# A weighted sum over eight experts on one core: the weights come in transfers of 121 and of 7 partitions instead of 128

## The chip, the core and the metric

The kernel runs on one core of a Trainium2 chip. The time is the device time of one execution in microseconds (us); lower is better. Seven executions of the kernel before took 707.96 to 708.42 us, with a median of 708.09 us.

## What is computed

```python
batch, seq, n_experts, expert_dim = 16, 1024, 8, 512
expert_outputs   # (16, 1024, 8, 512) float32
combine_weights  # (16, 1024, 8) float32

def reference(expert_outputs, combine_weights):
    weights = combine_weights[..., np.newaxis]
    return np.sum(expert_outputs * weights, axis=2).astype(np.float32)
```

There are 16 x 1024 = 16384 tokens. Each has eight rows of 512 numbers and eight weights, and its output is the weighted sum of its eight rows. The input is 268 MB, the output 33.6 MB, and the weights are 0.5 MB, so nearly all that moves is `expert_outputs`, once, and it is used once.

## The kernel before

**Tiling.** The tokens are laid on 128 partitions, 128 tokens on each. 120 of them are done in a loop, the last 8 (`TAIL`) behind it. The loop has 12 rounds (`ROUNDS`) of 10 tokens for each partition (`R`). The input of one round fills a buffer `ring` in SBUF, and it comes in three transfers (`CHUNKS`) of 4, 4 and 2 tokens for each partition: 8.4, 8.4 and 4.2 MB. A chunk of the next round overwrites the same place as soon as VectorE has used it.

**The order of transfers.** SyncE (`SP` in the profile) issues the loads in a fixed order, written out in `loads_and_last_stores`. Ahead of each load it waits for the semaphore `done`, which VectorE counts up for each finished token. After the first chunk of the first round, SyncE issues the two transfers of the weights: the 120 tokens of the loop (three runs of 1280 bytes for each partition, L113) and the 8 of the tail (256 bytes for each partition, L116). Both count up `w_in` when they land. Then come the rest of the loads, the eight loads of the tail (L119, one token each), and the last five stores (L99, L123). ScalarE (`ACT`) issues the eleven other stores from its own queue, one for each round (L99).

**The weights.** ScalarE waits for `w_in`, then copies the weights of each round from `w_t` to `w_c` (L145), two rounds in turn, and counts up `w_set`. In the tail it multiplies an identity matrix by a column of weights (L151), which TensorE uses.

**The sum.** VectorE does the loop: for each token a product (L204) and seven fused multiply-adds (L187), two tokens interleaved. Ahead of a round it waits for the weights and for the store of two rounds ago, and ahead of a chunk for its landing (all with L173). In the tail TensorE sums the first four experts of each token in PSUM (L163, with the diagonal matrices as weights) and VectorE adds the other four. VectorE waits for `w_in` once more before the tail.

**DMA engines.** Sixteen DMA engines serve the core. A transfer over 128 partitions is split into sixteen shares of eight partitions, each engine takes its share in the order of the queue, and adds one to the semaphore when its share has landed; the transfer has landed when sixteen have come.

## Time and profile before

| | |
|---|---|
| median of seven executions | 708.09 us (707.96 to 708.42) |
| the profiled execution: its own time | 707.74 us |
| its span in the profile | 705.9 us |
| VectorE busy | 628.2 us (89%) |
| TensorE, ScalarE, GpSimd busy | 33.4, 16.7, 0.7 us |
| DMA: moved, mean rate | 302.53 MB, 429 GB/s |
| packets on SyncE's queue (q1), ScalarE's (q10), instructions' (q14) | 7600, 1584, 2 |
| mean granted TensorE clock | 0.994 |

The span is the stretch that the profile shows; the 1.84 us between it and the execution's own time lie around it. The profiled execution is 0.35 us below the median of the seven. In the profile's rows of slices a digit is the share of time in tenths, 9 being 90% or more. A "packet" is what one DMA engine moves in one go: 64 KB of one partition for a chunk of four tokens, 20 KB for a store, 1280 bytes for a run of weights, 4 bytes for the count of a semaphore. The trace holds queue, start, duration and size of each packet and the time of each of the sixteen counts of a transfer, but not the number of the DMA engine.

### The profile page before, as it was taken

Reading aid. Unit: us, or ns where it says so; the run is one execution under the profiler, and the core shown is the slowest. Engines: PE = TensorE matmul, PEld = TensorE weight load, DVE = VectorE, ACT = ScalarE, POOL = GpSimd, SP = SyncE. Lnnn points to the kernel's source line nnn. Section 1 sums busy time; section 2 is a strip of 40 time slices with the busy share of each in tenths; the row PEclk is TensorE's granted clock in tenths of the full one; section 3 lists DMA queues with packets and bytes.
Section 4 is the critical chain, followed back from the end, with each engine's and each line's share of the span. In section 5 each row is a group of like instructions: output and inputs, shape, how many; then the busy total and the mean of one; then the engine's idle time right before and its main releaser. Section 6 shows DMA issues by size and latency. Waiting matters only on the chain. (4 is left out here: it accounts for less than half of the span.)

```text
span 705.9 us, 1388 instructions
## 1 busy us (share of the span) xinstructions
PE 33.4 (5%) x64; PEld 13.2 (2%) x64; DVE 628.2 (89%) x992; ACT 16.7 (2%) x45; POOL 0.7 (0%) x6
## 2 busy tenths in 40 slices
PE   0000000000000000000000000000000000000674
PEld 0000000000000000000000000000000000000221
DVE  0599989979979979979979989998997997997995
ACT  0000000000000000000000000000000000000221
POOL 0000000000000000000000000000000000000000
PEclk9999999999999999999999999999999999999998
DMA  9999999999999999999999999999999999999997
GB/s 408 394 472 420 401 429 447 412 446 420 450 431 451 431 405 446 436 424 470 434 396 454 417 425 436 472 395 467 420 446 416 427 430 457 434 432 402 429 430 331
DMA packets 9186, 302.53 MB, mean 429 GB/s; under 512 B 1120, under 2 KB 1504, under 8 KB 1888
## 3 DMA queue, kind: packets, MB, share of 16 engines
q1 hardware_dynamic: 7600, 273.68, 90.0%
q10 hardware_dynamic: 1584, 28.84, 9.5%
q14 instruction: 2, 0.02, 0.0%
HBM read 268.96 MB, written 33.55 MB: 429 GB/s over the span
## 5 line engine op out<-in xcount | busy, mean ns | idle before, releaser
L187 DVE SCALAR_TENSOR_TENSOR acc<-ring,w_c,acc 128x512 f32<-128x512 f32 x840 | 561.4, 744 | 0.0
L204 DVE TENSOR_SCALAR acc<-ring,w_c 128x512 f32<-128x512 f32 x120 | 52.6, 480 | 68.2 <-DVEq L173 68.2
L163 PE MATMUL ps<-ring,diag 128*128 128x512 f32 x64 | 33.4, 676 | 663.9 <-DMA ring<-in_expert_outputs_dram 663.8
L163 PEld LDWEIGHTS ps<-ring,diag 128*128 128x128 f32 x64 | 13.2, 214 | 683.2 <-DMA ring<-in_expert_outputs_dram 668.3
L187 DVE SCALAR_TENSOR_TENSOR acc<-ring,w_t,acc 128x512 f32<-128x512 f32 x24 | 17.6, 749 | 0.6
L145 ACT COPY w_c<-w_t 128x80 f32<-128x80 f32 x12 | 3.0, 258 | 560.0 <-DVE acc L187 537.7
L151 ACT ACTIVATE diag<-ident,w_t 128x128 f32<-128x128 f32 x32 | 12.4, 400 | 114.6 <-PE ps L163 60.4
L187 DVE SCALAR_TENSOR_TENSOR acc<-ring,w_t,ps 128x512 f32<-128x512 f32 x8 | 5.9, 742 | 3.4 <-PE ps L163 3.4
L145 ACT ACT_TABLE_LOAD x1 | 1.3, 1283 | 0.9 <-SPq L230 0.9
L129 POOL TENSOR_SCALAR_AFFINE_SELECT ident<-ident 128x128 f32<-128x128 f32 x1 | 0.3, 292 | 0.1
L128 POOL MEMSET ident<- 128x128 f32 x1 | 0.2, 204 | 0.5 <-SPq L230 0.5
L250 POOL MEMSET const-bfloat16-1.0<- 128x1 bf16 x1 | 0.1, 101 | 0.0
L250 POOL MEMSET const-uint8-127<- 128x1 uint8 x1 | 0.1, 101 | 0.0
L250 POOL MEMSET const-float32-0.0<- 128x1 f32 x1 | 0.1, 98 | 0.2 <-issue 0.2
L250 POOL MEMSET const-float32-1.0<- 128x1 f32 x1 | 0.1, 98 | 0.0
## 6 DMA issues: line engine op xcount, KB each, us to landing
ring<-in_expert_outputs_dram SPq DMA_DIRECT2D x12, 4096.0 KB, 34.4
out_dram<-acc ACTq DMA_DIRECT2D x11, 2560.0 KB, 26.7
ring<-in_expert_outputs_dram SPq DMA_DIRECT2D x8, 2048.0 KB, 30.1
out_dram<-acc SPq DMA_DIRECT2D x1, 2560.0 KB, 26.2
out_dram<-acc SPq DMA_DIRECT2D x1, 1024.0 KB, 16.4
out_dram<-acc SPq DMA_DIRECT2D x1, 512.0 KB, 9.5
out_dram<-acc SPq DMA_DIRECT2D x2, 256.0 KB, 5.4
w_t<-in_combine_weights_dram SPq DMA_DIRECT2D x1, 480.0 KB, 22.7
```

Source lines behind the costliest of these rows:

```text
L128: gpsimd.memset(ident, 0.0).then_inc(id_set, 1)
L129: gpsimd.affine_select(out=ident, in_=ident, compare_op=mybir.AluOpType.not_equal, fill=1.0, base=0, pattern=[[-1, P]], channel_multiplier ...
L145: scalar.copy(out=w_c[:, h * R : h * R + R], in_=w_t[:, n * R : n * R + R]).then_inc(w_set[h], 1)
L151: i = scalar.mul(out=diag[:, k % DIAGS], in_=ident, mul=w_t[:, LOOP + j, e : e + 1])
L163: tensor.matmul(ps[:, j], lhsT=diag[:, k % DIAGS], rhs=ring[:, j, e], start=e == 0, stop=e == pe_e[j] - 1,).then_inc(product, 1)
L187: return vector.scalar_tensor_tensor(out=acc[:, g], in0=ring[:, g % R, e], scalar=weight, in1=before, op0=mult, op1=add)
L204: i = vector.tensor_scalar_mul(out=acc[:, g], in0=ring[:, g % R, 0], scalar1=weight)
L250: nc = _bacc.Bacc("TRN2", target_bir_lowering=False, num_devices=1)
```

## The change

Each of the two transfers of the weights becomes two: one for partitions 0 to 120, and one for partitions 121 to 127. 121 partitions are split over eleven DMA engines with eleven partitions each, seven over seven engines with one each. The order on SyncE's queue is 121 partitions of the loop's weights, 121 of the tail's, 7 of the loop's, 7 of the tail's; they stand at the same place between the first and the second chunk. The two waits for `w_in` wait for 64 instead of 32. SyncE issues two more transfers; no other engine's instructions change.

```diff
                 if n == 0 and c == 0:
-                    sync.dma_start(
-                        out=w_t[:, 0:LOOP].rearrange("p (n m) e -> p n m e", m=M), in_=w_g
-                    ).then_inc(w_in, 16)
-                    sync.dma_start(out=w_t[:, LOOP:T_P], in_=w_x).then_inc(w_in, 16)
+                    for p in (slice(0, 121), slice(121, P)):
+                        sync.dma_start(
+                            out=w_t[p, 0:LOOP].rearrange("p (n m) e -> p n m e", m=M), in_=w_g[p]
+                        ).then_inc(w_in, 16)
+                        sync.dma_start(out=w_t[p, LOOP:T_P], in_=w_x[p]).then_inc(w_in, 16)
...
     def weights_and_stores(scalar):
-        scalar.wait_ge(w_in, 32)
+        scalar.wait_ge(w_in, 64)
...
         take(stored[0], 16)
-        vector.wait_ge(w_in, 32)
+        vector.wait_ge(w_in, 64)
```

## The prediction

> **What bounds the kernel now.** I read the page first, then the stretches, then the end packet by packet.

> ```profile
> span 705.9 us, 1388 instructions
> ...
> DMA  9999999999999999999999999999999999999997
> ...
> q14 instruction: 2, 0.02, 0.0%
> ...
> L204 DVE TENSOR_SCALAR acc<-ring,w_c 128x512 f32<-128x512 f32 x120 | 52.6, 480 | 68.2 <-DVEq L173 68.2
> ```

> The DMA row is full from the first slice to the last but one, while VectorE (DVE) stands still for 68.2 us ahead of the product that opens a token: it waits for chunks. The kernel lives on its DMA engines. The stretches say how tightly, and at the end something more:

> ```profile
> core 0: us, PE busy (x) PEld busy (x) DVE busy (x) ACT busy (x) POOL busy (x), PEclk, DMA share, GB/s
> 60.00:660.00 600.00, 1.69 (x2) 0.84 (x3) 556.89 (x885) 4.15 (x15) 0.00 (x0) 1.00 1.00 432
> ```
> ```profile
> 701.00:702.00 1.00, 0.00 (x0) 0.00 (x0) 0.00 (x0) 0.00 (x0) 0.00 (x0) 0.57 1.02 397
> 702.00:703.00 1.00, 0.00 (x0) 0.00 (x0) 0.00 (x0) 0.00 (x0) 0.00 (x0) 0.50 0.25 94
> 703.00:704.00 1.00, 0.00 (x0) 0.00 (x0) 0.00 (x0) 0.00 (x0) 0.00 (x0) 0.50 0.06 25
> ```

> A DMA share of 1.00 over 600 us leaves no engine idle. In the last but one microsecond of transfers the share is 0.06, which is 1/16: one engine still works and fifteen are done. I call it the late engine. Its last sixteen packets of 2 KB follow each other every 80 ns, from 702.80 to 704.09 us in the packet records, so it is not waiting for VectorE; it has a backlog. Fourteen others end by 702.55, one at 702.75. Nothing in the span ends later but the landing of its last packets (704.45) and 1.4 us of closing steps. The end is thus the total work of one DMA engine.

> Why is it late? The counts of the semaphores date it. The second chunk's sixteen counts lie within 0.57 us (43.13 to 43.70). Of the third, fifteen have come by 53.42 and one comes at 54.02. Of the last tail load, fifteen by 692.07 and one at 693.48. Two steps, and beside both lies one packet of the instruction queue:

> ```profile
> DMA packets 49, 1.58 MB, mean 527 GB/s; under 512 B 16, under 2 KB 16, under 8 KB 16
> ...
> q14 instruction: 1, 0.01, 0.7%
> ```
> ```profile
> DMA packets 122, 1.73 MB, mean 432 GB/s; under 512 B 16, under 2 KB 16, under 8 KB 16
> ...
> q14 instruction: 1, 0.01, 0.5%
> ```

> These are the DMA view's answers for 51 to 54 and 680 to 684 us. At 51.37 us an 8 KB fetch of instructions takes 0.33 us and the load packet beside it 1.88 us instead of 1.21: together 0.98 us. The second, at 681.05, raises the lag of the same engine (the distance of the last count from the median of the sixteen) from about 1.0 to 1.9 us. The late engine is the one that fetches instructions.

> Last, what the weights do at the start and who waits for them:

> ```profile
> 24.43 0.42 ACT L145 COPY w_c<-w_t 128x80 f32<-128x80 f32 x2 [22.25 <-DMA w_t<-in_combine_weights_dram]
> 25.07 0.88 DVE L204 TENSOR_SCALAR acc<-ring,w_c 128x512 f32<-128x512 f32 x2 [25.07 <-DVEq L173]
> ```
> ```profile
> 86.27 9.36 DVE L187 SCALAR_TENSOR_TENSOR acc<-ring,w_c,acc 128x512 f32<-128x512 f32 x14
> 97.91 0.88 DVE L204 TENSOR_SCALAR acc<-ring,w_c 128x512 f32<-128x512 f32 x2 [2.29 <-DVEq L173]
> ```

> VectorE begins when the weights are copied, then runs without a gap until 95.6, where it first waits for a chunk, for 2.29 us.

> **Part by part.** *The weights' share of an engine.* In the records each engine spends 24 packets of 1280 bytes, one every 52 ns (1.25 us), 8 of 256 bytes every 14 to 15 ns (0.11 us) and two counts (0.01 us): 1.37 us, the same on all sixteen, from the last packet of the first chunk to the first of the second. That is 0.17 us for a partition. By bytes alone (512 KB at the page's 429 GB/s) it would be 1.22 us, or 0.15 for a partition. I take 0.17, the measured one.

> *The new shares.* If the seven engines are among the eleven, seven engines carry 12 partitions, four carry 11 and five none. Twelve cost 12 x 0.17 + 4 x 0.006 = 2.06 us, 0.70 more than now (0.61 by bytes); eleven cost 1.88, 0.51 more (0.46); none is 1.37 less (1.22). If the seven are others, the most on one engine is still 12 and the least 1, which changes the relief to 1.2. The trace has no transfer of fewer than 128 partitions, so the split itself is the change's word.

> [...]

> *Two more transfers.* After the weights' count, the next packet starts 6 ns later (23.272 to 23.278 us in the records), so a transfer more in a queue that never runs dry costs its packets and about 6 to 9 ns for its count. I take 0.01 us an engine, counted above. The other bound is that each count is waited for before the next transfer's packets, about 0.3 to 0.7 us (last weight packet to landing, 23.8 to 24.41): no row shows such a wait, so it only widens the slower side.

> [...]

> *SyncE's queue.* Its two issues took 0.42 and 0.48 us; two more put the second chunk's issue from 2.37 to 3.3 us. The first chunk runs until 22.5, which hides it. With that cover gone it would cost 0.9.

> *The waits for `w_in`.* The last count moves from 24.41 to about 25.1 (0.70 later). Behind ScalarE's wait stand the copies and all its stores, behind those VectorE's start. The start moves to 25.8. It is hidden by the 2.29 us that VectorE waits at 95.6, and until then SyncE's loads queue several us ahead (the load issued at 45.2 begins at 52.3). Without that cover 0.70 would count. VectorE's second wait, before the tail, is long satisfied.

> *The end.* No engine idles, so a microsecond of packets more on the late engine is a microsecond at the end, and less is less until the next engine is the last. The sum hangs on one thing: how many partitions of weights the late engine gets. No view names the engine. By count, 7 of 16 engines get 0.70 more, 4 get 0.51 more, 5 get 1.37 less.

> **The forecast** is therefore the late engine among the eleven. The profiled 707.74 becomes 708.44 (twelve) or 708.25 (eleven); on the median, 0.35 above, 708.79 or 708.60. Weighted seven to four: 708.75, +0.09%. About 0.2% (1.42 us) is what a measurement of this kernel can tell from no change, so this is "the same". Its own range is 708.5 (0.46 by bytes) to 709.0.

> **The rivals.** *The late engine is one of the five without weights: faster, 707.25.* Its end comes at 704.09 - 1.37 = 702.72. Then others are last: the one at 702.75 becomes 703.45 with twelve partitions, 703.26 with eleven; if it too is relieved, those that ended by 702.29 to 702.55 end at 702.99 to 703.25. The gain is 0.64 to 1.10, to 707.0 to 707.45. For it: two fetches of 0.98 make exactly one engine late, and relief there is worth the whole step. Against it: five in sixteen.

> *One instruction fetch more, on the path: slower, 709.8.* SyncE gets two instructions more. A third packet of the instruction queue comes at 706.46, after the span; if it belongs to SyncE, it moves forward by two instructions, and what stands just ahead are the waits of the last stores. Price 0.98 if it falls before 704.8 us on the late engine, on top of 0.70: 708.09 + 1.68 = 709.8. It decides only if it hits the very engine that ends last. Against it: that packet lies 2 us behind the last wait.

> *The split does not happen:* if 121 partitions went over one engine, 121 x 0.17 = 20.6 us less its 1.4 now would end up late there: about 727 us. Nothing in the trace speaks for it or against it.

> **How the numbers follow.** Forecast 0.55; late engine relieved 0.37 (a little above five in sixteen: which engine fetches instructions need not be an even draw, and no view says); third fetch 0.04; no split 0.02; something else 0.02. The first two lie within 0.2%, so faster gets 0.02, same 0.92, slower 0.06. The range takes in both: 707.0 from the relief of 1.1, 709.0 from 0.70 with a small wait for the counts; 8% lies outside.

> **What would show it.** In the changed profile, five engines' first packets of the second chunk should start 1.4 us before the first of the others, and seven last, at 23.97 or later. Where the late engine stands is read at the end: a share of 0.06 until about 704.8 means that it carries weights, a share that falls from several engines near 703.2 that it was relieved. Two fetches, 0.98 each, should be there as before. I would be wrong if VectorE's first gap (2.29 us) grows, if the weights land over 1 us later, or if engines idle between chunks.

## The result and the profile after

The changed kernel takes 709.89 us (13 executions, 709.78 to 710.16) against 708.02 us before (33 executions): 1.87 us more, a ratio of 1.0027 with a 95% interval of 1.0020 to 1.0034. The forecast was 708.75, within 0.2%; the range ended at 709.0. The two profiled executions, 707.74 and 709.91 us, lie 2.17 us apart, since the one before was 0.28 us below its median.

The page of the changed kernel shows no new bound:

```profile
span 708.1 us, 1390 instructions
...
DMA  9999999999999999999999999999999999999997
...
q14 instruction: 2, 0.02, 0.0%
...
L205 DVE TENSOR_SCALAR acc<-ring,w_c 128x512 f32<-128x512 f32 x120 | 52.6, 480 | 70.4 <-DVEq L174 70.4
```

DMA is as full as before, VectorE's work is the same, and it stands still 2.2 us longer. The stretches, with their header, say that the long middle is untouched and that one engine still ends last, two microseconds later:

```profile
core 0: us, PE busy (x) PEld busy (x) DVE busy (x) ACT busy (x) POOL busy (x), PEclk, DMA share, GB/s
60.00:660.00 600.00, 0.00 (x0) 0.00 (x0) 557.80 (x885) 4.15 (x15) 0.00 (x0) 1.00 1.00 433
704.00:705.00 1.00, 0.00 (x0) 0.00 (x0) 0.00 (x0) 0.00 (x0) 0.00 (x0) 0.50 0.38 143
705.00:706.00 1.00, 0.00 (x0) 0.00 (x0) 0.00 (x0) 0.00 (x0) 0.00 (x0) 0.50 0.06 25
```

The fetches of instructions are there as before, in the DMA view's answers for 54 to 57 and 682 to 686 us, and in the packet records the load packets beside them last as long as they did (1.88 us at the first):

```profile
q14 instruction: 1, 0.01, 0.7%
```
```profile
q14 instruction: 1, 0.01, 0.5%
```

What has changed stands at the start. First the timeline of ScalarE and VectorE, whose last column is the idle time and what ended it:

```profile
27.56 0.42 ACT L146 COPY w_c<-w_t 128x80 f32<-128x80 f32 x2 [25.37 <-DMA w_t<-in_combine_weights_dram]
28.19 0.88 DVE L205 TENSOR_SCALAR acc<-ring,w_c 128x512 f32<-128x512 f32 x2 [28.19 <-DVEq L174]
```
```profile
100.21 0.88 DVE L205 TENSOR_SCALAR acc<-ring,w_c 128x512 f32<-128x512 f32 x2 [1.46 <-DVEq L174]
```

The weights come 3.1 us later, not 0.7. VectorE still waits before its chunk at 98.7 us, for 1.46 us instead of 2.29, so its late start costs nothing. What costs is the rate at which the weights move. Both kernels between 22.55 and 23.15 us, when the engines with weights move little else; before, then after:

```profile
22.55:23.15 0.60, 0.00 (x0) 0.00 (x0) 0.00 (x0) 0.00 (x0) 0.00 (x0) 1.00 1.05 393
```
```profile
22.55:23.15 0.60, 0.00 (x0) 0.00 (x0) 0.00 (x0) 0.00 (x0) 0.00 (x0) 1.00 0.80 181
```

Sixteen engines moved 393 GB/s, 24.6 each. Eleven move 181, or 16.5 each, while five hold 64 KB packets that started earlier (a view counts a packet where it starts). In the packet records a run of 1280 bytes took 55 ns in all 384 cases before; now the median is 102, the mean 96 and the longest 234. The 64 KB packets that the five engines started at 22.15 to 22.31 took 3.9 to 4.5 us instead of 2.42.

The counts of the second chunk tell who is late: five come at 43.89 to 44.23 us and eleven at 45.96 to 46.49, against 43.13 to 43.70 for all sixteen before. Even the five engines without weights are later than before. At the last tail load the five are at 691.5 to 691.8, ten at 693.5 to 694.2, and one at 695.67.

### The profile page after: what moved, and what is told of

It reads as the page before. It is cut to its first block, busy times and chain, and to the rows that moved or that the text cites. A ratio compares the mean times of both kernels' runs of the same rounds, so it can differ in the third digit from the quotient of the medians.

```text
span 708.1 us, 1390 instructions
## 1 busy us (share of the span) xinstructions
PE 31.6 (4%) x64; PEld 12.4 (2%) x64; DVE 628.1 (89%) x992; ACT 16.7 (2%) x45; POOL 0.7 (0%) x6
## 2 busy tenths in 40 slices
DMA  9999999999999999999999999999999999999997
## 5 line engine op out<-in xcount | busy, mean ns | idle before, releaser
L205 DVE TENSOR_SCALAR acc<-ring,w_c 128x512 f32<-128x512 f32 x120 | 52.6, 480 | 70.4 <-DVEq L174 70.4
L164 PE MATMUL ps<-ring,diag 128*128 128x512 f32 x64 | 31.6, 642 | 667.8 <-DMA ring<-in_expert_outputs_dram 667.8
```

The costliest lines, as they stand in the source:

```text
L164: tensor.matmul(ps[:, j], lhsT=diag[:, k % DIAGS], rhs=ring[:, j, e], start=e == 0, stop=e == pe_e[j] - 1,).then_inc(product, 1)
L205: i = vector.tensor_scalar_mul(out=acc[:, g], in0=ring[:, g % R, 0], scalar1=weight)
```

## The experiments

I had three theories for the slow packets. A: engines that write to the same group of SBUF partitions at once share its rate, and the shares of a 128-partition transfer keep them apart. B: engines in different work, 64 KB beside 1280 bytes, disturb each other. C: each added transfer has a fixed price, 0.9 us.

**Four transfers of 128 partitions.**

```diff
-                    for p in (slice(0, 121), slice(121, P)):
+                    for i in range(LOOP // M):
                         sync.dma_start(
-                            out=w_t[p, 0:LOOP].rearrange("p (n m) e -> p n m e", m=M), in_=w_g[p]
+                            out=w_t[:, i * M : i * M + M], in_=w_g[:, i]
                         ).then_inc(w_in, 16)
-                        sync.dma_start(out=w_t[p, LOOP:T_P], in_=w_x[p]).then_inc(w_in, 16)
+                    sync.dma_start(out=w_t[:, LOOP:T_P], in_=w_x).then_inc(w_in, 16)
```

> Four transfers of the weights, as in the changed kernel, but each over 128 partitions (three of 40 tokens, one of the tail's 8). Theory A (several DMA engines write to the same group of partitions, which happens as soon as the shares are not those of 128 partitions): no loss, weight packets of 55 ns, 708.0 to 708.1 us. Theory B (engines that move 64 KB packets beside engines that move weights disturb each other): the same, since all engines are equal. Theory C (each added transfer has a fixed price, 0.9 us from the 1.87 us of two): two transfers added, 709.9 us.

707.86 us against 707.93, a ratio of 0.9998 (0.9989 to 1.0007), every packet 55 ns. Theory C falls: as many transfers as the change, at no price.

**Halves of 64, then 112 and 16.** Here all sixteen engines were meant to have equal shares.

```diff
-                    for p in (slice(0, 121), slice(121, P)):
+                    for p in (slice(0, 64), slice(64, P)):
```

> The weights in halves of 64 and 64 partitions; sixteen engines with four partitions each in each of four transfers, so all engines are equal again. Theory A: engines share destinations two by two within a half, weight packets of about 102 ns as in the changed kernel, the weights take 1.25 us more on every engine: 709.3 us. Theory B: 55 ns, 708.0 us. Theory C: 709.9 us with packets of 55 ns.

> The weights over 112 and 16 partitions: sixteen engines with seven and with one, eight on each as before, but not the eight of a 128-partition transfer. Theory A: weight packets of about 100 ns for most of the 112 partitions, 1.2 us more: 709.2 us, no engine ahead of the others. Theory B: packets of 55 ns, 708.0 us. Theory C: 709.9 us.

The halves took 708.28 us, a ratio of 1.0006 (0.9997 to 1.0015), 112 and 16 took 707.87, 0.9999 (0.9990 to 1.0008). Neither time can be told from that of the kernel before; the packets can. Their mean was 84 ns for halves (median 88) and 67 ns for 112 and 16 (median 61). Theory B by itself falls, for no engine was ahead and it gave 55 ns. The size that I gave theory A was too large, and the end shows less than the weights lose, of which more below.

**120 and 8**, the same edit with 120: meant for fifteen engines with eight partitions and one without.

> The weights over 120 and 8 partitions: fifteen engines with eight, the first eight of them with one more, one engine without. The smallest version of what the change does. By shares alone: the late engine, one of the first eleven by the changed kernel's trace, gets 0 or 0.17 us more: 708.0 to 708.2 us. Theory A: weight packets of 60 to 90 ns on average, 0.3 to 0.8 us more at the weights, of which some 0.5 us may come back at the first store as with 112 and 16: 707.9 to 708.6 us.

708.86 us, a ratio of 1.0013 (1.0004 to 1.0022), packets of 82 ns on average. By shares it should have been 708.2 at most.

**The weights alone.** The second chunk is held back until they have landed, in the changed kernel, in the one before, and in the changed kernel with runs of the input in the place of weights:

```diff
                 if n:
                     sync.wait_ge(done, (n - 1) * R + r + m)
+                if n == 0 and c == 1:
+                    sync.wait_ge(w_in, 64)   # 32 in the kernel before
```

> The changed kernel, and the second chunk is issued only when all the weights have landed, so nothing but weights moves beside weights. The time is not the point (it loses some us in which the engines stand idle); the packets are. Theory A: weight packets still about 100 ns once the engines are under way, weights about 2.5 to 4 us an engine. Theory B: 55 ns throughout, 2.05 us on the engines with twelve partitions. Theory C: 55 ns, and a gap between the transfers.

> The kernel before, and the second chunk is issued only when all the weights have landed: the control to the same change of the changed kernel, whose weight packets took 76 ns on average with nothing beside them. Theory A (engines that write to the same group of partitions at once share its rate): 55 ns, since a 128-partition transfer gives each engine its own group. Rival (standing alone is what slows them): about 76 ns.

> The changed kernel with the second chunk issued when the weights have landed, but what is loaded as weights comes from the input: runs of the same 1280 and 256 bytes out of rows 655 KB apart (the output is then another sum). Theory A: destinations as in the changed kernel, so again about 76 ns. Rival A2: rows far apart, so 55 ns.

Between 22.6 and 22.9 us, the kernel before and then the changed one, both with the chunk held back:

```profile
22.60:22.90 0.30, 0.00 (x0) 0.00 (x0) 0.00 (x0) 0.00 (x0) 0.00 (x0) 1.00 1.07 397
```
```profile
22.60:22.90 0.30, 0.00 (x0) 0.00 (x0) 0.00 (x0) 0.00 (x0) 0.00 (x0) 1.00 0.81 183
```

The changed kernel's packets took 76 ns on average, 55 in the kernel before, and 75 with rows 655 KB apart in HBM. So 121 partitions were slow with nothing beside them but the end of the first chunk, and no faster with source rows far apart. The further step from 76 to 96 ns came with the 64 KB packets beside them. Whether that is theory B, or theory A with 64 KB packets in the same groups of partitions, no run separates.

**Eight partitions, neighbours or four apart.** Here the kernel before loads the loop's weights in sixteen transfers of eight partitions, one partition for each of eight engines. The tail's weights stay one transfer, the waits count to 272, and the second chunk is held back as above:

```diff
                 if n == 0 and c == 0:
-                    sync.dma_start(
-                        out=w_t[:, 0:LOOP].rearrange("p (n m) e -> p n m e", m=M), in_=w_g
-                    ).then_inc(w_in, 16)
+                    for i in range(16):
+                        p = slice(8 * i, 8 * i + 8)                                    # one run: neighbours
+                        p = slice(32 * (i // 4) + i % 4, 32 * (i // 4) + 32, 4)        # the other: four apart
+                        sync.dma_start(
+                            out=w_t[p, 0:LOOP].rearrange("p (n m) e -> p n m e", m=M), in_=w_g[p]
+                        ).then_inc(w_in, 16)
...
```

> The loop's weights in sixteen transfers of eight partitions, four apart (0, 4, 8 to 28, and so on), one partition for each of eight engines; the second chunk waits until all have landed. Theory A: eight different groups of partitions, so no two engines share one: packets of 55 ns, though no transfer has 128 partitions. Rival A2 (the source: rows that lie near each other in HBM, read by several engines at once): slow, and as slow as with eight neighbouring partitions. Rival A3 (any transfer of fewer than 128 partitions is slow): slow.

> The same sixteen transfers of eight partitions, but neighbouring ones (0 to 7, 8 to 15, and so on). Theory A: eight engines write to two groups of four partitions, so a group's rate of about 27 GB/s (64 KB in 2.42 us) is shared by four: 1280 bytes in about 190 ns. Rivals A2 and A3: the same as with the eight partitions four apart.

Four apart: 55 ns for each of the 384, so eight partitions at a time were as fast here as 128 (rival A3 falls). Neighbours: 57.6 ns on average, 125 at most, where I had expected 190. That is a miss. The engines came out of the first chunk up to 0.7 us apart, and one engine's share of such a transfer is 0.17 us, so I suppose that they were several transfers, and so several groups, apart; this is argued. The next pair takes that way out with long packets: the second chunk of the kernel before, 8.4 MB, in the same two patterns.

```diff
+                if n == 0 and c == 1:
+                    for i in range(16):
+                        p = ...            # as above, neighbours or four apart
+                        if i == 15:
+                            sync.wait_ge(parts, 240)
+                        sync.dma_start(
+                            out=ring[p, r : r + m], in_=x_g[0, 0, p, g : g + m]
+                        ).then_inc(loaded[c] if i == 15 else parts, 16)
+                    continue
```

> The kernel before, with its second chunk (8.4 MB) loaded in sixteen transfers of eight neighbouring partitions, one for each of eight engines. The packets are now 64 KB, so engines cannot drift onto other partitions between two packets as they may have with 1280 bytes. Theory A (a group of partitions takes only about 27 GB/s, which the engines that write to it share): four engines in each of two groups, so the first packets of this chunk last up to four times 2.42 us, near 9.7 us, and later ones less as the engines drift apart. Rival A3 (it is the weights' small runs, not the destinations): 2.4 to 3.1 us. The time of the kernel grows in both, since eight engines load what sixteen did.

> The same sixteen transfers, with partitions four apart (0, 4, 8 to 28, and so on). Theory A: each engine has its own group, 2.42 us for a packet, 3.0 to 3.3 at most for the first. Rival A3: the same as with neighbouring partitions.

The same bytes by the same eight engines between 26 and 56 us, neighbours and then four apart:

```profile
26.00:56.00 30.00, 0.00 (x0) 0.00 (x0) 19.74 (x32) 0.00 (x0) 0.00 (x0) 1.00 0.46 52
```
```profile
26.00:56.00 30.00, 0.00 (x0) 0.00 (x0) 19.17 (x30) 0.00 (x0) 0.00 (x0) 1.00 0.49 210
```

For the splits there is only an estimate of the mean packet of 1280 bytes. It takes groups of four neighbours, as above. It gives each engine an equal run of neighbouring partitions in each transfer, with 64 KB packets behind them as in a 128-partition transfer. It lets a group pass the 27.1 GB/s measured here, shared equally by the engines that write to it, and starts the engines up to 0.5 us apart, by chance, eight times over.

| split | measured | estimate, four neighbours |
|---|---|---|
| 121 and 7, second chunk held back | 76 ns | 57 ns |
| 121 and 7 | 96 ns | 63 ns |
| 120 and 8 | 82 ns | 60 ns |
| halves | 84 ns | 56 ns |
| 112 and 16 | 67 ns | 62 ns |

The estimate comes near for 112 and 16 and is 19 to 33 ns too low for the others. So groups of four neighbours alone do not account for them: what else the engines share in these splits, or disturb, was not shown, and the step from 76 to 96 ns stays open with it. Which partitions an engine takes is assumed in it, for the records do not name them.

**What comes back at the first store.** Each slow split loses more at the weights (the median count of the second chunk against the kernel before) than at the end (the last count of the last tail load). For 121 and 7 the median is that of the eleven engines.

| split | at the weights | at the end | back |
|---|---|---|---|
| 112 and 16 | 0.58 us | 0.06 us | 0.52 us |
| halves | 1.02 us | 0.60 us | 0.42 us |
| 120 and 8 | 1.38 us | 0.98 us | 0.40 us |
| 121 and 7 | 2.75 us | 2.19 us | 0.56 us |

Each row is of one traced execution, and executions of the kernel before lie up to 0.8 us apart, so these differences are rough. The packet records show where to look. Around its first store the kernel before has 64 KB packets of 2.5 to 3.3 us, between 76.8 and 81.3 us, 0.70 us for an engine on average; four transfers of 128 partitions have 0.50. None of the four splits in the table has one. Two runs asked what they are, and a third what becomes of them when the weights stand elsewhere:

```diff
# the first store six tokens later
-        queue.wait_ge(done, (n + 1) * R)
+        queue.wait_ge(done, (n + 1) * R + (6 if n == 0 else 0))
# the tail's weights (or both transfers) issued by ScalarE at the start
-                    sync.dma_start(out=w_t[:, LOOP:T_P], in_=w_x).then_inc(w_in, 16)
+        scalar.dma_start(out=w_t[:, LOOP:T_P], in_=w_x).then_inc(w_in, 16)
         scalar.wait_ge(w_in, 32)
```

> The kernel before, with the first store issued six tokens later (about 108 us instead of 75.5 us), which nothing waits for. It asks where the 0.7 us go that the kernel before loses in its 64 KB packets between 76.8 and 81.3 us, and the changed kernel does not. If the first store on its queue causes them: they move to about 109 us or vanish. If it is the data or the phase of the engines: they stay at 77 to 81 us.

> The kernel before, with the tail's weights (32 KB) issued by ScalarE at the start, so that its queue is used long before the first store. The kernel before loses 0.5 to 0.7 us in its 64 KB packets at the first store; the changed kernel and three other splits do not. Theory D (it is the first use of ScalarE's queue): the slow packets at 77 to 81 us are gone, 707.4 us. Theory E (it is the first write to HBM beside the loads, or the phase of the engines): they stay, 708.0 us.

> The kernel before, with both transfers of the weights issued by ScalarE at the start, beside the first chunk instead of between the first and the second; 128 partitions, so each engine keeps its own group. By theory A packets stay at 55 ns, though 64 KB packets run in the same engines' queues; the bytes are the same. Theory D: slow packets at the first store gone, 707.4 us. Theory E: 708.0 us.

With the later store (issued at 105.7 us) the slow packets moved to 108.1 to 110.0 us, 0.54 us an engine, and the time was 707.74: they belong to the first store. With the tail's weights on ScalarE's queue they stayed, 0.66 us at 76.6 to 81.5, and the time was 708.39, a ratio of 1.0006 (0.9997 to 1.0015): it is not the first use of that queue. Why the four splits are spared them stays open. Slow weights alone do not spare a kernel: 121 and 7 with the second chunk held back has weights of 76 ns and these packets too, 0.66 us an engine.

The last run missed by far: 732.24 us, a ratio of 1.0345 (1.0330 to 1.0359). Its DMA view gives the time from issue to landing in the last column, 22.7 us for the same transfer in the kernel before:

```profile
w_t<-in_combine_weights_dram ACTq DMA_DIRECT2D x1, 480.0 KB, 51.1
```
```profile
53.37 0.42 ACT L144 COPY w_c<-w_t 128x80 f32<-128x80 f32 x2 [50.17 <-DMA w_t<-in_combine_weights_dram]
```

The packets of 1280 bytes still took 55 ns, but each engine took one of them and then one of 64 KB from the other queue, some fifteen turns of 2.47 us, and then a few turns of 1.27 us with packets of 32 KB. VectorE began at 54.0 us.

## Why the prediction was wrong

**The step that failed is the price of a share.** The waits, the path and the engine that ends last were right; the term was too small. "That is 0.17 us for a partition" was measured on the shares of 128-partition transfers, 55 ns for a run of 1280 bytes, and it went unchanged into "Twelve cost 12 x 0.17". Followed back packet by packet from its fetch at 54.19 us, the late engine began the second chunk at 25.50 us, where it had begun at 23.51: 1.99 us more instead of 0.51 to 0.70. With the 1.37 us of before that makes 3.36 us for eleven or twelve shares, 0.28 to 0.31 us each. In the place of the constant price the runs put one that depends on the split: a run of 1280 bytes took 96 ns on average here and 67 to 84 in the other three splits, instead of 55. The late engine's first 64 KB packet then took 3.28 us instead of 2.44, which the sum did not have: 2.83 us by the second packet (25.94 and 28.77). About 0.6 of it came back, mostly at the first store, where the kernel before loses time and this one does not, and its last landing moved from 704.45 to 706.64, by 2.19. The range missed for the same reason: its upper end, 709.0, was twelve shares at the old price with a small wait for counts, and that supposes that sixteen engines are sixteen roads. A slip of addition is too small to matter: 708.79 and 708.60, weighted seven to four, give 708.72 and not 708.75.

**The late engine is among the eleven: right.** The forecast counted seven engines with twelve partitions, four with eleven and five with none, and no run before the result showed that the seven are among the eleven. The changed kernel's counts do. `w_in` has 36 between 25.64 and 27.53 us, twice eleven and twice seven, beside one for each transfer at 1.91 to 3.36, before any weights move. Five engines are ahead from 43.9 us to the end, and the one that fetches is not one of them. So five carry no weights and the seven are among the eleven, as the forecast had taken it, and the rival that the late engine is relieved fell. Whether it has eleven partitions or twelve, the records do not say. The relief of 1.37 us was meant for engines that never were last, and even their second chunk came 0.5 to 0.8 us later.

**Two more transfers cost nothing: right**, by the four transfers of 128 partitions (707.86 us against 707.93). No fixed price appeared, nor the wait for counts that I had kept as a bound.

**SyncE's issues and VectorE's start are hidden: right**, though the start moved by 3.1 us; VectorE's gap shrank by 0.83, from 2.29 to 1.46. I had named weights that land over 1 us later as a sign against me, and they landed 3.1 us later, at 27.53 instead of 24.41.

**A third fetch, no split:** neither came. The third packet of the instruction queue stayed behind the span, at 708.64 us, and the eleven and five engines are plain in the counts.

**The end is the work of one DMA engine: right**, and it is why two microseconds at 25 us are still there at 706.

## What to carry to other kernels

Before a transfer is split by partitions, ask which partitions each DMA engine writes at the same moment, not only how many bytes it carries: eight engines on eight neighbouring partitions moved 52 GB/s here between 26 and 56 us and 210 on partitions four apart, and the profile showed them as equally busy (a DMA share of 0.46 and 0.49). Take GB/s beside the DMA share to see it. Where the transfers end last on one engine, find out which engine that is before shifting work: here five others were relieved of their weights, and the end came 2.19 us later.

## What the runs showed that I had not expected

- Eight engines on eight neighbouring partitions: 9.15 to 9.17 us for 64 KB, against 2.42 with partitions four apart.
- In these kernels a 64 KB packet took 2.5 to 3.5 us on nearly every engine when it was the first after a pause or after slow weights; in three of the five kernels that waited for their weights the last engine to start took 2.42.
- With the weights on ScalarE's queue the engines took turns between two queues by packets, not by bytes: 480 KB of weights took 51.1 us beside loads in 64 KB packets, 22.7 us in line with them.
- Around the first store the loads' packets were slow, by 0.5 to 0.8 us an engine in most of these kernels and not at all in the four splits.
